# One split instruction for up to four pieces of weights instead of two, in a two-layer decoder trunk on one Trainium2 core

## The chip, the core and the metric

The kernel runs on one core of one Trainium2 chip. The metric is device time in microseconds of one launch, that is, of the whole two-layer trunk for one sequence of 256 tokens. All data are float32 in memory. Engine names in what follows: PE is TensorE (matmuls; PEld are its weight loads), DVE is VectorE, ACT is ScalarE, SP is the engine whose queue issues the transfers here.

## What is computed

The reference is a decoder trunk of two layers, cut here to what matters:

```python
for layer in range(2):
    shift, scale, gate = modulation(c, ada_w[layer])        # matrix-vector products with silu(c)
    h = x * (1 + scale) + shift
    y = rglru_mixer(h)  if layer == 0 else nsa_mixer(h)      # recurrent block / sparse attention
    x = layer_norm(ALPHA * x + (1 + gate) * y)
    # the same once more with y = square(relu(h @ w1)) @ w2
```

Each layer has a mixer with its input and output projections and an MLP of 2048 to 8192 to 2048. There are four sub-layers in all (mixer, MLP, mixer, MLP), each with its own modulation (three products of a 2048-vector with a 2048 by 2048 matrix) and its own layer norm. Some 610 MB of weights are read once each.

## The kernel before

**Weights as a stream.** All weights come as one list of units (`Item`), each 128 partitions by 2048 columns of float32 (1 MB), in the order in which they are needed. `prefetch` (L95 to L107) issues one transfer a unit on SP's queue into one of six raw buffers. `pump` (L109 to L146) takes the next unit that has arrived, and does what its kind asks: a unit of modulation weights ("a") goes through one multiply-and-sum on DVE (L120, 2048 columns) and its buffer is free again; a unit of matmul weights ("w") holds four **pieces** of 512 columns, and is split.

**The split.** A float32 product is made of three matmuls with rounded parts (L193 to L195): high by high, high by low, low by high. So each weight is needed as a high part `whi`, a rounded copy made on ACT (L135), and a low part `wlo`, the rest, made on DVE (L136: raw minus `whi`). Both live in a ring of 16 pieces. The ring has two counters: `prod`, how many pieces have been split, and `cons`, how many PE has used up. A split may be issued when its pieces fit: its last piece may be at most 16 ahead of `cons`. Before the change one pair of instructions makes two pieces (1024 columns), and a unit takes two pairs:

```python
w = min(1024, it.width)
s = it.p0 + 2 * it.group
if s + 2 > self.cons + RING:
    return
```

**Matrix products.** `gemm_ws` takes a piece as the stationary operand (12 matmuls of 256 columns a piece), `gemm_as` the activations (3 matmuls of 512 columns a piece and token tile; there are two token tiles of 128 rows). With `stagger` the first token tile goes over all 16 pieces of a chunk before the second one starts, and only the second gives pieces back to the ring.

**The order of the work.** The program is recorded in one pass: a counter of estimated time decides when `pump` emits a split and when side tasks (normalization, gates, activations) take their next step. A scheduler then orders each engine's instructions, and each engine runs its own in that order. An instruction that waits holds up all that stand behind it on its engine.

**Places named below.**
- `modulate` (L447 to L462): four tiles of 128 features are scaled on ACT (L454), then split like the weights: high part on ACT (L496), low part on DVE (L497). What L454 needs (`hA`, `hB`) comes from L427 to L436 on DVE, right behind the L120s.
- The first sub-layer's input is made in five groups of 4, 4, 4, 2 and 2 feature tiles (`GROUPS0`), the second's in four groups of 4 (`GROUPS1`). Each group has its L120s, then its modulation, then four units of weights (`w_part`); those of the two groups of 2 hold two pieces each. `gemm_ws_outer` runs the group's 16 (or 8) pieces.
- `proj` (L602 to L662) makes the output projections; its `task` multiplies by the gate (L632), adds the residual (L637), takes statistics (L638). `ln_task` (L504 to L572) follows for each token tile: L509, L511 (ACT), L517 to L530, then L534 (ACT) and L540 normalize, L549 transposes on PE, L553 copies (ACT), or L561 and L563 modulate. There are four layer norms; the first ends near 379 us of the profile, the second lies around 1115 to 1141 us, the third around 1544 to 1566 us, the last at the end.

Of the kernel before, what the change touches and what calls it, by code (L numbers as in the profile page):

```python
# [33 lines left out]
NS2 = 6  # L34
LNACT = (0, 2)
# [14 lines left out]
class Builder:  # L50
# [58 lines left out]
    def pump(self):  # L109
        nc = self.nc  # L110
        while self.pi < len(self.items):
# [15 lines left out]
            else:  # L127
                w = min(1024, it.width)
                s = it.p0 + 2 * it.group
                if s + 2 > self.cons + RING:  # L130
                    return
                src = r[:, 1024 * it.group:1024 * it.group + w]
                hi = self.whi[:, s % RING:s % RING + 2, :].rearrange("p a b -> p (a b)")[:, :w]
                lo = self.wlo[:, s % RING:s % RING + 2, :].rearrange("p a b -> p (a b)")[:, :w]
                nc.scalar.activation(hi, src, AF.Copy)  # L135
                nc.vector.tensor_tensor(out=lo, in0=src, in1=hi.bitcast(F32), op=OP.subtract)  # L136
                self.prod = s + 2
                it.group += 1
                if 2 * it.group < it.pieces:
                    continue  # L140
# [45 lines left out]
    def head(self, kind):  # L186
        """The unit that is next in the stream, as it came."""
# [22 lines left out]
    def gemm_ws_outer(self, act, dones, kinds, groups):  # L210
        """Several chunks of columns side by side, a few tiles of the contraction at a time."""
# [14 lines left out]
    def gemm_as(self, act, done, stagger=None, kind="g"):  # L226
# [13 lines left out]
        # the first token tile runs ahead of the second by as many tiles of weights as the ring holds  # L240
# [37 lines left out]
def build(ctx, tc, a, out):  # L278
# [30 lines left out]
    # silu(c), on every partition  # L309
# [112 lines left out]
    def make_ss(s, k0=0, k1=16):  # L422
        """h = zn * hA + hB, with zn the normalized rows before sub-layer s (its input where s is 0)."""
# [20 lines left out]
    def modulate(s, k0, k1, rows, A):  # L444
        """Up to four feature tiles of the transposed rows become the two parts of the modulated ones."""
# [59 lines left out]
    def ln_task(s, z, t, stats, A, fin=None, rows=None):  # L505
        """Normalizes the rows of token tile t and, with A, makes sub-layer s+1's modulated rows, transposed
        (or with rows, the transposed rows alone; or with fin, the last layer norm's w and b, the output)."""
# [400 lines left out]

    tok = [None, None]

    # compressed keys and values
    kc = const.tile([128, 4, 15], F32, name="kc")
    vc = B.t2([15, 4, 128])

# [325 lines left out]
```

## Time and profile before

| | before |
|---|---|
| three runs | 2290.78 us median (2289.36 to 2290.9) |
| the profiled execution | span 2292.0 us, from the first to the last instruction (no other time is listed for it) |
| PE busy | 2198.1 us, 96% |
| DVE busy | 1672.3 us, 73% |
| ACT busy | 1057.2 us, 46% |
| mean granted TensorE clock | 0.987 |
| split instructions | 721 on ACT (L135), 721 on DVE (L136) |
| transfers | 623.95 MB, mean 272 GB/s |

The profile is of one execution. Busy times overlap, so a share says nothing by itself of what a stage waits for. PE's 2198.1 us leave 93.9 us in which PE was idle.

### The profile page before, as it was taken

What the parts mean: (1) busy time and instruction counts of PE and PEld (TensorE: products, weight loads), DVE (VectorE), ACT (ScalarE), POOL (GpSimd) and SP (SyncE); (2) the same over time, 40 slices, a digit from 0 to 9 for tenths busy, and PEclk for the clock granted to TensorE, in tenths of its full rate; (3) what the DMA queues carried; (4) which work ended last, traced back from release to release, by engine and by line L of the source; (5) the groups of instructions that cost most, each with busy time, mean ns of one, the idle gap of its engine ahead of it and who ended that gap; (6) DMA issues with size and microseconds to landing.
All of it is one profiled execution on the core that took longest, in us unless ns stands there. A gap on an engine that the chain in (4) does not pass through costs nothing.

```text
span 2292.0 us, 33881 instructions
## 1 busy us (share of the span) xinstructions
PE 2198.1 (96%) x13970; PEld 1966.2 (86%) x13970; DVE 1672.3 (73%) x1987; ACT 1057.2 (46%) x1383; POOL 0.2 (0%) x4
## 2 busy tenths in 40 slices
PE   4799998989999999999999999999999999999997
PEld 3798977978998998998789988788989989988986
DVE  8899999886777767778887688668766444454456
ACT  2356644364453453444443355536544534443541
POOL 0000000000000000000000000000000000000000
PEclk9899999999999999999999999999999999999999
DMA  9987888988878878788689775356788555555561
GB/s 371 411 331 286 338 328 322 373 346 341 306 302 321 298 273 310 294 302 319 234 292 349 293 272 214 132 192 219 281 308 307 190 190 189 191 184 185 208 250 37
DMA packets 98218, 623.95 MB, mean 272 GB/s; under 512 B 10909, under 2 KB 13405, under 8 KB 26896
## 3 DMA queue, kind: packets, MB, share of 16 engines
q1 hardware_dynamic: 98064, 621.80, 72.5%
q8 instruction: 109, 1.79, 0.3%
q14 instruction: 45, 0.37, 0.0%
HBM read 613.30 MB, written 8.45 MB: 271 GB/s over the span
## 4 chain that ended last, share of the span: by engine, by line
PE 84%; DVE 11%; ACT 2%; issue 2%; DMA 1%; DVEq 0%; SPq 0%; ACTq 0%
PE g L195 26%; PE g L194 26%; PE g L193 26%; DVE raw L120 5%; DVE wlo L136 2%; PE m L1124 1%; PE m L1090 1%; ACT whi L135 1%; DMA raw<-in_lru_in 1%; DVE s L801 1%; PE m L929 1%; PE m L1116 0%; PE m L1127 0%; DVE s L497 0%; ACT s L454 0%
## 5 line engine op out<-in xcount | busy, mean ns | idle before, releaser
L136 DVE TENSOR_TENSOR wlo<-raw,whi 128x1024 fp32r<-128x1024 f32 x721 | 872.1, 1222 | 512.4 <-ACT whi L135 510.9
L135 ACT ACTIVATE whi<-raw 128x1024 fp32r<-128x1024 f32 x721 | 754.7, 1057 | 911.7 <-PE g L195 454.2
L193 PE MATMUL g<-s,whi 128*128 128x256 f32 (+1 forms) x2768 | 781.1, 283 | 51.6 <-ACT s L496 50.0
L194 PE MATMUL g<-s,whi 128*128 128x256 f32 (+1 forms) x2768 | 780.4, 282 | 5.1 <-DVE s L497 5.1
L195 PE MATMUL g<-s,wlo 128*128 128x256 f32 (+1 forms) x2768 | 780.6, 283 | 3.2 <-DVE wlo L136 3.2
L193 PEld LDWEIGHTS g<-s,whi 128*128 128x128 f32 (+1 forms) x2768 | 523.1, 189 | 59.1 <-ACT s L496 53.0
L193 PE MATMUL g<-whi,s 128*128 128x512 f32 x1376 | 547.4, 398 | 5.4 <-ACT s L496 5.4
L194 PE MATMUL g<-wlo,s 128*128 128x512 f32 x1376 | 544.9, 396 | 0.0
L195 PE MATMUL g<-whi,s 128*128 128x512 f32 x1376 | 544.6, 396 | 0.3 <-DVE s L497 0.3
L194 PEld LDWEIGHTS g<-s,whi 128*128 128x128 f32 (+1 forms) x2768 | 525.8, 190 | 8.9 <-DVE s L497 6.8
L195 PEld LDWEIGHTS g<-s,wlo 128*128 128x128 f32 (+1 forms) x2768 | 525.1, 190 | 4.8 <-DVE wlo L136 3.8
L120 DVE SCALAR_TENSOR_TENSOR raw<-raw,one,cond 128x2048 f32<-128x2048 f32 x192 | 447.7, 2345 | 19.1 <-DMA raw<-in_ada 18.9
L193 PEld LDWEIGHTS g<-whi,s 128*128 128x128 f32 x1376 | 258.9, 188 | 70.2 <-ACT s L496 7.4
L195 PEld LDWEIGHTS g<-whi,s 128*128 128x128 f32 x1376 | 258.7, 188 | 64.8 <-DVE s L497 2.2
L194 PEld LDWEIGHTS g<-wlo,s 128*128 128x128 f32 x1376 | 258.9, 188 | 62.0 <-issue 0.8
L454 ACT ACTIVATE s<-s,hB,hA 128x256 f32<-128x256 f32 x32 | 16.7, 590 | 120.9 <-DVE hA L430 80.4
L194 PE MATMUL m<-s,whi 128*128 128x256 f32 x256 | 71.1, 278 | 0.0
L195 PE MATMUL m<-s,wlo 128*128 128x256 f32 x256 | 71.1, 278 | 0.0
L193 PE MATMUL m<-s,whi 128*128 128x256 f32 x256 | 70.8, 279 | 0.2 <-ACT whi L135 0.2
L497 DVE TENSOR_TENSOR s<-t,s 128x512 fp32r<-128x512 f32 x78 | 52.8, 685 | 1.5 <-ACT s L496 1.3
L675 ACT ACTIVATE t<-g 128x512 f32<-128x512 f32 x58 | 33.9, 588 | 34.7 <-PE g L195 34.7
L193 PEld LDWEIGHTS m<-s,whi 128*128 128x128 f32 x256 | 47.8, 188 | 0.5 <-ACT whi L135 0.4
(189 smaller groups left out, 1048.6 us busy)
## 6 DMA issues: line engine op xcount, KB each, us to landing
raw<-in_mlp_w SPq DMA_DIRECT2D x256, 1024.0 KB, 5.0
raw<-in_ada SPq DMA_DIRECT2D x192, 1024.0 KB, 6.6
raw<-in_lru_in SPq DMA_DIRECT2D x28, 1024.0 KB, 8.4
raw<-in_nsa_kv SPq DMA_DIRECT2D x24, 1024.0 KB, 5.3
raw<-in_lru_out SPq DMA_DIRECT2D x16, 1024.0 KB, 6.3
raw<-in_nsa_q SPq DMA_DIRECT2D x16, 1024.0 KB, 6.5
raw<-in_nsa_out SPq DMA_DIRECT2D x16, 1024.0 KB, 4.9
t<-in_lnrow SPq DMA_DIRECT2D x24, 256.0 KB, 6.2
```

The lines of the kernel that those rows point to most:

```text
L120: nc.vector.scalar_tensor_tensor(r, r, self.one, self.cond, op0=OP.mult, op1=OP.mult, accum_out=it.col)
L135: nc.scalar.activation(hi, src, AF.Copy)
L136: nc.vector.tensor_tensor(out=lo, in0=src, in1=hi.bitcast(F32), op=OP.subtract)
L193: mm(out, lhi, rhi, start=start, stop=False, skip_group_check=True)
L194: mm(out, lhi, rlo, start=False, stop=False, skip_group_check=True)
L195: mm(out, llo, rhi, start=False, stop=stop, skip_group_check=True)
L497: V.tensor_tensor(out=lo, in0=src, in1=hi.bitcast(F32), op=OP.subtract)
L675: SC.activation(r2, banks[b], AF.Relu)
L801: V.scalar_tensor_tensor(o[:, sh:], p[:, :256 - sh], tap(i, j), o[:, sh:], op0=OP.mult, op1=OP.add)
L929: T.matmul(hv, r[:, 128 * l:128 * l + 128], x[:, :, h:15 + h, l], start=(h == 0 and l == 0), stop=(h == 1 and l == 15))
L1090: T.matmul(ps, qT[:, h, 128 * t:128 * t + 128], kT[g // 2][:, g % 2, :, 0:K], start=True, stop=True)
L1124: T.matmul(po, vt[br][:, kt, 128 * g:128 * g + 128], pT[:, br, kt], start=first, stop=False)
```

## The change

A constant `WIDE = 4` is new. A split now covers `n` pieces: up to four, but not past the end of the unit and not past the end of the ring. Its instructions are up to 2048 columns wide, and it is issued when all its `n` pieces fit into the ring. (The diff also drops comments, so that line numbers after the change are 1 to 3 higher.)

```diff
+WIDE = 4
...
             else:
-                w = min(1024, it.width)
-                s = it.p0 + 2 * it.group
-                if s + 2 > self.cons + RING:
+
+                s = it.p0 + it.group
+                n = min(WIDE, it.pieces - it.group, RING - s % RING)
+                if s + n > self.cons + RING:
                     return
-                src = r[:, 1024 * it.group:1024 * it.group + w]
-                hi = self.whi[:, s % RING:s % RING + 2, :].rearrange("p a b -> p (a b)")[:, :w]
-                lo = self.wlo[:, s % RING:s % RING + 2, :].rearrange("p a b -> p (a b)")[:, :w]
+                w = min(512 * n, it.width - 512 * it.group)
+                src = r[:, 512 * it.group:512 * it.group + w]
+                hi = self.whi[:, s % RING:s % RING + n, :].rearrange("p a b -> p (a b)")[:, :w]
+                lo = self.wlo[:, s % RING:s % RING + n, :].rearrange("p a b -> p (a b)")[:, :w]
                 nc.scalar.activation(hi, src, AF.Copy)
                 nc.vector.tensor_tensor(out=lo, in0=src, in1=hi.bitcast(F32), op=OP.subtract)
-                self.prod = s + 2
-                it.group += 1
-                if 2 * it.group < it.pieces:
+                self.prod = s + n
+                it.group += n
+                if it.group < it.pieces:
                     continue
```

In the built program the 720 splits of 1024 columns on each engine become 316 of 2048 and 88 of 1024; the one of 768 (`nsa_g`, the attention's branch gates) stays. Of the 88, eight belong to the two small groups of `GROUPS0`. The other 80 come behind `nsa_g`, which has two pieces: from there on every fourth unit lies across the end of the ring and is split in two halves.

The order of the instructions moves with it. First place: **DVE, the first group of the first sub-layer** (`hA` is the modulation's scale, `s` are the activations, `wlo` and `whi` the ring). Before:

```order
L430 TENSOR_SCALAR hA_91<-mod_87 128x4
L136 TENSOR_TENSOR wlo<-raw,whi 128x1024
L497 TENSOR_TENSOR s_224<-s_187,s_223 128x1024
L136 TENSOR_TENSOR wlo<-raw,whi 128x1024 x7
L120 SCALAR_TENSOR_TENSOR raw,mod_87<-raw,one,cond 128x2048 x4
```

and with the change:

```order
L433 TENSOR_SCALAR hA_91<-mod_87 128x4
L139 TENSOR_TENSOR wlo<-raw,whi 128x2048
L500 TENSOR_TENSOR s_224<-s_187,s_223 128x1024
L139 TENSOR_TENSOR wlo<-raw,whi 128x2048 x3
L121 SCALAR_TENSOR_TENSOR raw,mod_87<-raw,one,cond 128x2048 x4
```

The activations' low part still stands behind the first split, which is now twice as wide; ACT's order is the same (L454, one `whi`, L496, the other `whi`). The second and third group, and the third and fourth of the second sub-layer, read alike.

Second place: **DVE, the first layer norm, second token tile** (`z` is named `s` here; L632, L637, L638 and L509 belong to the second tile). Before:

```order
L540 TENSOR_SCALAR s_2895<-s_2895,mv,r 128x512
L136 TENSOR_TENSOR wlo<-raw,whi 128x1024
L632 TENSOR_TENSOR s_2895<-g_2832,s_2546 128x512
L637 SCALAR_TENSOR_TENSOR s_2895<-t_2829,s_2895 128x512
L638 BN_STATS stats_2351<-s_2895 128x6
L509 BN_AGGR mv<-stats_2351 128x2
L517 TENSOR_SCALAR var<-mv 128x1
```

and with the change:

```order
L543 TENSOR_SCALAR s_2807<-s_2807,mv,r 128x512
L139 TENSOR_TENSOR wlo<-raw,whi 128x2048
L635 TENSOR_TENSOR s_2807<-g_2746,s_2478 128x512
L640 SCALAR_TENSOR_TENSOR s_2807<-t_2743,s_2807 128x512
L641 BN_STATS stats_2295<-s_2807 128x6
L512 BN_AGGR mv<-stats_2295 128x2
L139 TENSOR_TENSOR wlo<-raw,whi 128x2048
L520 TENSOR_SCALAR var<-mv 128x1
```

Before, the group's eight narrow splits all stood ahead of the second tile's L632; now three wide ones do, and the fourth stands between its L509 and L517. In the first tile's part, the first narrow split stood between L637 and L638; the first wide one stands behind L638, L509 and L517.

Third place: **DVE, the third layer norm**, from the first low part of the first token tile (L497) to the second tile's gate (L632). Before:

```order
L497 TENSOR_TENSOR s_12652<-t_12646,s_12651 128x4x128
L136 TENSOR_TENSOR wlo<-raw,whi 128x1024
L497 TENSOR_TENSOR s_12672<-t_12666,s_12671 128x4x128
L136 TENSOR_TENSOR wlo<-raw,whi 128x1024
L497 TENSOR_TENSOR s_12689<-t_12683,s_12688 128x4x128
L136 TENSOR_TENSOR wlo<-raw,whi 128x1024
L497 TENSOR_TENSOR s_12708<-t_12702,s_12707 128x4x128
L632 TENSOR_TENSOR s_12607<-g_12558,s_12272 128x512
```

and with the change:

```order
L500 TENSOR_TENSOR s_12210<-t_12204,s_12209 128x4x128
L139 TENSOR_TENSOR wlo<-raw,whi 128x2048
L500 TENSOR_TENSOR s_12230<-t_12224,s_12229 128x4x128
L139 TENSOR_TENSOR wlo<-raw,whi 128x1024
L500 TENSOR_TENSOR s_12247<-t_12241,s_12246 128x4x128
L139 TENSOR_TENSOR wlo<-raw,whi 128x1024
L500 TENSOR_TENSOR s_12264<-t_12258,s_12263 128x4x128
L635 TENSOR_TENSOR s_12167<-g_12118,s_11844 128x512
```

Here one of three narrow splits became a wide one, so 1024 columns more stand between the first low part (L497 before, L500 now) and the second tile's gate (L632 before, L635 now). On ACT, ahead of the first L496 of this norm, three narrow `whi` behind L534 became two wide ones.

## Rows read from the trace of the kernel before

**Rows 1.** Busy time by stretch: stretch, length, engines, PEclk, DMA share, GB/s.
```profile
0.00:160.00 160.00, 111.23 (x804) 103.94 (x805) 141.85 (x200) 56.91 (x76) 0.20 (x4) 0.95 0.95 377
160.00:345.00 185.00, 178.37 (x1141) 161.31 (x1140) 183.24 (x198) 119.28 (x159) 0.00 (x0) 0.99 0.84 316
345.00:480.00 135.00, 116.49 (x792) 109.03 (x791) 122.90 (x148) 53.84 (x68) 0.00 (x0) 0.91 0.86 335
480.00:2292.00 1812.00, 1792.05 (x11239) 1591.97 (x11237) 1224.31 (x1445) 827.21 (x1081) 0.00 (x0) 1.00 0.69 254
1320.00:1480.00 160.00, 159.42 (x1015) 133.01 (x1015) 128.64 (x314) 86.52 (x227) 0.00 (x0) 1.00 0.58 212
```

**Rows 2.** PE's own waits: who waited for whom, us in total, times, longest.
```profile
PE g L193 <- ACT s L496: 55.4, 12, 25.9
PE m L549 <- ACT s L534: 8.7, 3, 3.9
PE g L195 <- DVE wlo L136: 3.2, 3, 2.4
```

**Rows 3.** Groups of instructions by form: busy us, mean ns | idle before, releasers.
```profile
L136 DVE TENSOR_TENSOR wlo<-raw,whi 128x1024 fp32r<-128x1024 f32 x720 | 871.2, 1222 | 511.8 <-ACT whi L135 510.3
L135 ACT ACTIVATE whi<-raw 128x1024 fp32r<-128x1024 f32 x720 | 753.9, 1058 | 911.1 <-PE g L195 454.2 <-PE g L194 381.2 <-DMA raw<-in_lru_in 29.7
L120 DVE SCALAR_TENSOR_TENSOR raw<-raw,one,cond 128x2048 f32<-128x2048 f32 x192 | 447.7, 2345 | 19.1 <-DMA raw<-in_ada 18.9
L497 DVE TENSOR_TENSOR s<-t,s 128x512 fp32r<-128x512 f32 x78 | 52.8, 685 | 1.5 <-ACT s L496 1.3
L496 ACT ACTIVATE s<-t 128x512 fp32r<-128x512 f32 x78 | 47.6, 624 | 0.1
```

**Rows 4.** Timeline, first group of the first sub-layer: start us, us, instruction [idle before].
```profile
37.13 1.04 ACT L135 ACTIVATE whi<-raw 128x1024 fp32r<-128x1024 f32 x1
38.20 1.23 DVE L136 TENSOR_TENSOR wlo<-raw,whi 128x1024 fp32r<-128x1024 f32 x1 [3.09 <-ACT whi L135]
39.02 6.72 ACT L135 ACTIVATE whi<-raw 128x1024 fp32r<-128x1024 f32 x7
40.48 8.03 DVE L136 TENSOR_TENSOR wlo<-raw,whi 128x1024 fp32r<-128x1024 f32 x7
```

**Rows 5.** Timeline, first layer norm: the splits behind the first token tile, L517 of the second.
```profile
362.01 1.06 ACT L135 ACTIVATE whi<-raw 128x1024 fp32r<-128x1024 f32 x1 [11.54 <-PE g L195]
363.41 1.06 ACT L135 ACTIVATE whi<-raw 128x1024 fp32r<-128x1024 f32 x1 [0.34 <-PE g L195]
...
363.10 1.23 DVE L136 TENSOR_TENSOR wlo<-raw,whi 128x1024 fp32r<-128x1024 f32 x1 [1.07 <-ACT whi L135]
364.24 0.69 DVE L638 BATCH_NORM_STATS2 stats<-s 128x6 f32<-128x512 f32 x1
...
377.29 0.15 DVE L517 TENSOR_SCALAR var<-mv 128x1 f32<-128x1 f32 x1
```

**Rows 6.** Timeline, groups of the second sub-layer: DVE's waits at the splits.
```profile
404.97 1.23 DVE L136 TENSOR_TENSOR wlo<-raw,whi 128x1024 fp32r<-128x1024 f32 x1 [1.10 <-ACT whi L135]
407.89 1.23 DVE L136 TENSOR_TENSOR wlo<-raw,whi 128x1024 fp32r<-128x1024 f32 x1 [1.70 <-ACT whi L135]
...
467.33 1.23 DVE L136 TENSOR_TENSOR wlo<-raw,whi 128x1024 fp32r<-128x1024 f32 x1 [0.70 <-ACT whi L135]
```

**Rows 7.** Timeline, third layer norm: PE's wait in the second token tile.
```profile
1569.55 0.50 PE L193 MATMUL g<-whi,s 128*128 128x512 f32 x1 [0.69 <-ACT s L496]
```

**Rows 8.** Busy time by stretch of L136 alone: stretch, length, DVE busy (count), PEclk, DMA, GB/s.
```profile
0.00:160.00 160.00, 37.37 (x32) 0.95 0.95 377
160.00:345.00 185.00, 72.32 (x62) 0.99 0.84 316
345.00:480.00 135.00, 40.33 (x34) 0.91 0.86 335
1320.00:1480.00 160.00, 37.11 (x31) 1.00 0.58 212
```

## The prediction

> **What bounds the kernel now.** I read first the busy time by stretch [rows 1]. PE's columns give its idle time: 160.00 - 111.23 = 48.8 us in the first stretch (0 to 160), 6.6 in the second (160 to 345), 18.5 in the third (345 to 480) and 20.0 in the 1812 us that follow. So for four fifths of the span PE is the bound, and DVE, busy 1224 of 1812 us there, may save microseconds that no one collects. Only 73.9 us ahead of 480 and 20.0 behind it are open to a change that leaves the matmuls alone. The second view is PE's own waits [rows 2]: 55.4 us for the activations' high part (L496), 8.7 us for a layer norm (L534), but only 3.2 us for a split low part. PE seldom waits for a split as such. It waits for the short chains that make the next activations, and these stand on ACT and DVE between the splits. The third view is the cost of the splits by form [rows 3]: on both engines nearly all the idle time ahead of a split is a wait, DVE's for `whi`, ACT's for PE to give pieces back. Last I read the timelines at those chains [rows 4 to 7].
>
> **What a wide split costs.** No instruction of before is a 2048-column split, so its time comes from two widths of alike work. On DVE 512 columns take 685 ns (L497) and 1024 take 1222 (L136), so 512 more cost 537, and 2048 take 1222 + 2 x 537 = 2296 ns. On ACT 624 and 1058 give 434 for 512, and 2048 take 1926 ns [rows 3]. The nearest bound above is L120, which works through 2048 columns in 2345. Two narrow ones don't cost 2 x 1222 = 2444 in a row, for they overlap: seven took 8.03 us on DVE, a pitch of (8.03 - 1.22)/6 = 1.135, and 6.72 on ACT, 0.943 [rows 4]. The second half of a wide one adds 1.074 and 0.868. So a pair merged saves 0.061 us on DVE and 0.075 on ACT. Without overlap it would save DVE 2444 - 2296 = 148 ns, the upper end.
>
> The 316 merged pairs take 316 x 0.061 = 19 us off DVE. Of these pairs some 60 lie ahead of 480 us: 32 narrow low parts up to 160 of which eight stay, 62 and 34 behind them [rows 8], so 12 + 31 + 17. The rest lie under PE. I price the saving there at nothing: the work that hides it is PE's, which uses a piece in about 1.5 us (1812 us for the other 592 narrow splits, two pieces each), while up to 12 of 16 pieces, some 18 us of matmuls, stand ready when a unit of four is split. A wide pair takes 1.9 + 2.3 us. If that cover went, each unit would cost PE up to 4.2 us, and the waits for low parts, 3.2 us now, would show it.
>
> **What it costs where the cover is thin.** Where a chain waits for the first split of a group, it now waits for all four pieces: `whi` ends 0.868 later, and what stands behind `wlo` on DVE, the activations' low part among it, another 1.074 later.
>
> *First three groups, first sub-layer (0 to 160).* DVE sits idle until the first `whi` (3.09 us ahead of 38.20) and then works without a gap [rows 4]. It starts 0.87 later and wins 4 x 0.061 = 0.24 back over the group's four units: +0.63. The next group's L120s queue behind it, and PE waits for them by way of L454 and L496. Three groups: **+1.9**. The lower end is 0, since DMA is 95% busy there [rows 1] and L120 waits 18.9 us for its data [rows 3]. The upper is 3 x 1.94 = 5.8, if PE feels both delays in each group.
>
> The Trainium skill ("Perfetto Trace Analysis", section "Optimizing Scalar/DVE Operations") has a rule that speaks against the change: where Scalar or Vector are not saturated but cause bubbles on other engines, breaking up instructions may let work complete sooner. By it all fronts below would be losses; the 3.09 us for which DVE sits idle agree with it.
>
> *Recurrent block (160 to 345).* DVE is busy 183.24 of 185 us. Some 7 merged pairs lie on its chain to the stretch's end: **-0.4**. The ends are -1.9 (31 x 0.061) and +1, a wide split ahead of one short operation.
>
> *First layer norm and second sub-layer (345 to 480).* The first split behind the first token tile had to wait for two pieces, until 362.01; the second for two more, until 363.41 [rows 5]. A wide one waits for four: +1.40, and its `whi` is 0.87 longer. Against that L638 (0.69) and one L517 (0.15) now run in the gap instead of behind the split, and four units win 0.24: **+1.2** (0.9 to 1.7). In the second group DVE waits twice for `whi`, 1.10 and 1.70 us [rows 6]. Each wait becomes 0.87 longer, less 0.24: **+1.5**; PE is still at work on the group before, but the third group's L120s queue behind it. The third group is like those above: **+0.6**. In the fourth DVE waits 0.70 for `whi` ahead of the low part [rows 6], and PE's own start hangs on both: 0.87 + 1.07, less some 0.2 of first matmuls that need no low part: **+1.7**. Together **+5.0**. The ends: 1.0, if PE and DMA (86% busy) hide all but one front, and 7.
>
> *Second and third layer norm.* In the second, three splits leave the first tile's chain and as many columns come to stand ahead of the second tile's gate: **0** (-0.9 to +1). In the third PE already waits 0.69 us for the second tile's L496 [rows 7], so a delay of that chain goes straight to PE. The first tile's L496 comes later by the longer `whi` ahead of it, 0.87, and 1024 more columns stand ahead of L632, 1.07: **+1.9** (0 to 3). The last norm has no splits beside it.
>
> Sum: 1.9 - 0.4 + 5.0 + 0 + 1.9 = **+8.4 us**. The profiled span of 2292.0 becomes 2300.4. That execution is 1.2 us longer than the median 2290.78, so on the median the forecast is **2299.2 us**. A measurement of this kernel can tell about 0.2%, 4.6 us, from no change; slower begins at 2295.4, faster below 2286.2.
>
> **Rivals.**
>
> *The fronts are hidden.* For it: the DMA share is 0.95, 0.84 and 0.86 in the three early stretches [rows 1], and L120 waits for data [rows 3]; if a late unit of weights ends most groups, DVE's 0.6 us matter to nobody, and a chain that starts late only turns idle time behind it into work. Against it: L120's waits are 18.9 us, PE's for L496 are 55.4. With the lowest ends of the early groups, 0 + 1.0, and about 1 from the third norm: 2290.78 + 2 = about 2293, no difference.
>
> *Grouping pays (the other side).* The place is 160 to 345 us and the groups of DVE work about it, where DVE is saturated, 183.24 of 185 [rows 1]. If narrow splits don't overlap there, since L120s and other operations stand between them, each pair saves 148 ns: 60 x 0.148 = 8.9 us, and if the fronts cost less than some 2 us, the time is 2290.8 - 8.9 + 2 = about 2284. It decides from about 6.6 us of net gain. Against it: PE is idle for only 6.6 us in the stretch where DVE is full, the seven splits in a row show the overlap plainly, and in the other two stretches DVE waits just where the split became longer.
>
> Such a rule is in the Trainium skill too (the same page and section): grouping into larger operations can improve throughput if the engine is saturated. DVE's 183.24 of 185 us fit its condition, PE's 20.0 us of idle time behind 480 leave it nothing there.
>
> *Attention suffers too.* From 1320 to 1480 us PE is busy 159.42 of 160 us, and DVE 128.64 [rows 1], with 31 narrow splits among its short chains [rows 8]. About 15 wide ones take their place; if half of these stand ahead of a chain that PE needs, 7 or 8 x 1.07 = some 8 us on top: about 2307. Against it: PE has only 0.6 us of waits there, so something else has covered chains that already stood behind 1.22 us splits and 2.35 us L120s.
>
> That the change does less than it says I leave out: the built program has 316 wide splits.
>
> **How the numbers follow.** The forecast, 2295.4 to 2306 with the fronts in full or for the most part, 0.55. Fronts hidden 0.27. Grouping pays 0.10. Attention suffers 0.08. Slower by over 0.2%: 0.55 + 0.08 = 0.63; within 0.27; faster 0.10. The ends of the terms add up to 0 - 1.9 + 1.0 - 0.9 + 0 = -1.8 and 5.8 + 1 + 7 + 1 + 3 = 17.8, but five ends do not come together; I take 2289.0 (the low ends) to 2306.0, which leaves out the faster rival, the worse one, and little else: about 2 in 10.
>
> **What would show it.** In the changed profile: L136's successor at 2048 columns near 2296 ns on DVE and 1926 on ACT; more than 2345 would mean that each unit costs more than two narrow splits. PE's idle time from 0 to 480 us should grow from 73.9 to about 80.4, with PE's wait for L496 up from 55.4; behind 480 from 20.0 to about 22. DVE's wait ahead of the first low part of a group should grow from 3.09 to about 3.96. In the first norm, the first wide `whi` should start where the second narrow one did, 1.4 us later. PE's waits for low parts should stay near 3.2. The forecast is wrong if the groups end at the same time as before although their first split ends later (then DMA or L120 ended them), if PE's idle time shrinks between 160 and 345 by more than 2 us, or if PE idles between 1320 and 1480.

## The result, and the profile after the change

The change made the kernel slower, by about half a per cent: 2302.73 us (2301.98 to 2305.72, four runs) against 2290.84 us, ratio 1.0053, 95% interval 1.0038 to 1.0067. Beside other runs of before it was measured once more (e8 below): 2301.85 us against 2291.73, ratio 1.0044 (1.0031 to 1.0057), which is +10 us. The forecast was 2299.2 us, from 2289.0 to 2306.0, and slower with 0.63. The profiled execution took 2301.98 us with a span of 2300.2; the forecast for the span was 2300.4.

Busy time by stretch of the changed kernel, with the columns of [rows 1]:

```profile
0.00:160.00 160.00, 110.94 (x796) 103.64 (x797) 139.21 (x185) 55.19 (x62) 0.20 (x4) 0.94 0.96 377
160.00:345.00 185.00, 178.18 (x1138) 161.90 (x1137) 181.63 (x170) 114.74 (x129) 0.00 (x0) 0.98 0.83 312
345.00:480.00 135.00, 113.56 (x752) 105.15 (x751) 117.32 (x128) 51.16 (x51) 0.00 (x0) 0.89 0.86 330
480.00:2300.20 1820.20, 1799.22 (x11289) 1597.41 (x11288) 1202.74 (x1192) 787.49 (x826) 0.00 (x0) 1.00 0.70 253
```

DVE is less busy in every stretch, ACT too, and PE is idle longer: 49.1, 6.8, 21.4 and 21.0 us instead of 48.8, 6.6, 18.5 and 20.0. These windows cut at fixed times and the later ones hold work that had been in the one before, so the delays below tell more. No window cuts the whole span: PE was idle for 93.9 us of it before and for 98.3 with the change. The cost of the splits by form, as in [rows 3]:

```profile
L139 DVE TENSOR_TENSOR wlo<-raw,whi 128x2048 fp32r<-128x2048 f32 x316 | 722.3, 2290 | 480.6 <-ACT whi L138 480.4
L138 ACT ACTIVATE whi<-raw 128x2048 fp32r<-128x2048 f32 x316 | 603.6, 1915 | 817.9 <-PE g L198 393.0 <-PE g L197 359.3 <-DVE s L626 11.0
```

A wide split takes 2290 ns on DVE and 1915 on ACT (forecast 2296 and 1926). PE's own waits, beside [rows 2] (L196 to L198 are what L193 to L195 were, L499 was L496, L552 was L549, L537 was L534):

```profile
PE g L196 <- ACT s L499: 57.4, 10, 26.7
PE m L552 <- ACT s L537: 9.0, 2, 6.9
PE g L196 <- ACT whi L138: 6.3, 7, 1.1
PE g L198 <- DVE wlo L139: 4.0, 1, 4.0
PE g L197 <- DVE s L500: 1.3, 1, 1.3
```

The last row stands for this one of before:

```profile
PE g L194 <- DVE s L497: 5.1, 6, 1.5
```

The wait for the activations' high part grew from 55.4 to 57.4. The third row, seven waits of about 1 us for a high part, is new but for one wait of 0.5 us. In exchange these waits for the activations' low part, six in before, came down to one. Now the timeline of the first group, beside [rows 4]:

```profile
37.20 1.89 ACT L138 ACTIVATE whi<-raw 128x2048 fp32r<-128x2048 f32 x1
39.95 5.50 ACT L138 ACTIVATE whi<-raw 128x2048 fp32r<-128x2048 f32 x3
...
39.13 2.29 DVE L139 TENSOR_TENSOR wlo<-raw,whi 128x2048 fp32r<-128x2048 f32 x1 [3.94 <-ACT whi L138]
42.47 6.69 DVE L139 TENSOR_TENSOR wlo<-raw,whi 128x2048 fp32r<-128x2048 f32 x3
```

DVE idles 3.94 us ahead of the group's first low part, not 3.09; the forecast said 3.96. Three wide ones in a row take 6.69 us, a pitch of (6.69 - 2.29)/2 = 2.20, against 2 x 1.135 = 2.27 for narrow pairs: 0.07 each, where 0.061 was forecast. The first layer norm, beside [rows 5], then the second group of the second sub-layer, beside [rows 6], and the third norm, beside [rows 7]:

```profile
365.99 1.91 ACT L138 ACTIVATE whi<-raw 128x2048 fp32r<-128x2048 f32 x1 [12.08 <-PE g L198]
...
367.94 2.29 DVE L139 TENSOR_TENSOR wlo<-raw,whi 128x2048 fp32r<-128x2048 f32 x1 [2.11 <-ACT whi L138]
...
406.69 2.29 DVE L139 TENSOR_TENSOR wlo<-raw,whi 128x2048 fp32r<-128x2048 f32 x1 [1.84 <-ACT whi L138]
...
414.29 1.23 DVE L500 TENSOR_TENSOR s<-s,s 128x1024 fp32r<-128x1024 f32 x1 [2.69 <-ACT s L499]
...
1562.30 0.50 PE L196 MATMUL g<-whi,s 128*128 128x512 f32 x1 [1.17 <-ACT s L499]
1577.69 0.50 PE L196 MATMUL g<-whi,s 128*128 128x512 f32 x1 [1.74 <-ACT s L499]
```

The first of the two waits of the third norm, in before:

```profile
1555.39 0.51 PE L193 MATMUL g<-whi,s 128*128 128x512 f32 x1 [0.65 <-ACT s L496]
```

PE's work is 2.58 us late when it comes to the first norm, so 365.99 answers to 363.41, to the hundredth where the second narrow split had started. In the second group DVE waits 1.84 and 2.69 us instead of 1.10 and 1.70, 1.73 more in all, where the forecast had 2 x 0.87. But they are not the same waits. The split at 406.69 now stands ahead of the modulation's `hA` and `hB` (L437 to L439), which in before were done by 402.73, ahead of the first of these waits; and the second wait is that of the activations' low part for its high part. In the third norm the second tile's wait is 1.74 instead of 0.69.

Since PE executes the same 13970 matmuls in both kernels, each can be matched by name and occurrence, and the difference of the two start times is PE's delay. This table gives what the delay grows by in each stretch (stretches by the times of before; worked out from the traces, each kernel against the profile of before):

| us, by stretch | to 165 | to 345 | to 490 | to 1165 | to 1310 | to 1545 | to 1600 |
|---|---|---|---|---|---|---|---|
| the change | +1.84 | +0.74 | +4.79 | -1.62 | -0.73 | +1.37 | +1.75 |
| the change again (e8) | +1.58 | +1.30 | +4.32 | -1.62 | 0.00 | +0.70 | +1.74 |
| before again (e4) | +0.13 | +0.14 | -0.62 | +0.66 | -0.87 | +0.17 | +0.01 |
| narrow groups (e1) | -0.03 | +1.80 | +0.56 | -1.62 | -0.88 | +1.37 | +1.73 |
| wide groups only (e2) | +1.82 | 0.00 | +4.05 | -0.80 | -0.15 | -0.36 | -0.58 |
| pairs (e3) | +0.18 | +0.36 | -0.40 | -1.00 | -1.00 | +1.33 | -0.58 |
| wide on ACT (e5) | +2.64 | +0.52 | +5.15 | +0.01 | +0.80 | +0.84 | +3.35 |
| wide on DVE (e6) | +1.82 | -0.81 | +3.50 | +1.33 | -0.97 | +0.42 | +2.73 |
| short first unit (e7) | +2.55 | +2.37 | -0.84 | -1.02 | -0.88 | +0.18 | +0.01 |
| first unit narrow (e9) | +0.40 | +0.40 | +1.70 | -1.44 | -0.74 | +1.44 | +1.73 |
| wide recurrent block (e10) | +0.23 | +2.35 | +0.66 | -0.99 | -0.88 | +0.74 | +0.03 |
| wide MLPs (e11) | +0.16 | +0.16 | +0.20 | -1.00 | -0.88 | +0.74 | +0.03 |
| 512 columns (e12) | +3.46 | +1.26 | +1.05 | -1.03 | -1.17 | +0.44 | +0.11 |

Each row is one execution. The two of before differ by up to 0.9 us in a stretch, so a smaller difference between two rows says little. From 490 to 1600 us the kernels e10 and e11, which are narrow through both norms and attention, gain 1.1 us on the profile of before, but so they do on e4, the same kernel profiled again. That 1.1 us lies in the second norm, at the transposes of its second token tile. In before, e4 and e11:

```profile
1141.51 3.38 PE L549 MATMUL m<-ident,s 128*128 128x128 f32 x16 [2.86 <-ACT s L534]
1141.36 3.11 PE L549 MATMUL m<-ident,s 128*128 128x128 f32 x16 [2.86 <-ACT s L534]
1142.22 1.97 PE L560 MATMUL m<-ident,s 128*128 128x128 f32 x16 [2.86 <-ACT s L545]
```

After the same wait of 2.86 us the same 16 transposes take 3.38 or 3.11 us in before and 1.97 in e11, and in the change too. TensorE's granted clock has two levels, 1.2 and 2.4 GHz, and PEclk is its mean as a share of the higher one. From 1137 to 1160 us it is 0.85 in before, 0.78 in e4, 0.93 in e11 and in the change. Why it fell ahead of these transposes in some kernels and not in others is not shown.

### The profile page after: what moved, and what is told of

It is laid out like the page before. It is cut to its first block, busy times and chain, and to the rows that moved or that the text cites. A ratio compares the mean times of both kernels' runs of the same rounds, so it can differ in the third digit from the quotient of the medians.

```text
span 2300.2 us, 32804 instructions
## 1 busy us (share of the span) xinstructions
PE 2201.9 (96%) x13970; PEld 1968.1 (86%) x13970; DVE 1640.9 (71%) x1671; ACT 1008.6 (44%) x1067; POOL 0.2 (0%) x4
## 4 chain that ended last, share of the span: by engine, by line
PE 85%; DVE 10%; ACT 2%; issue 2%; DMA 1%; DVEq 0%; SPq 0%; ACTq 0%
PE g L198 26%; PE g L197 26%; PE g L196 26%; DVE raw L121 5%; DVE wlo L139 2%; PE m L1127 1%; PE m L1093 1%; ACT whi L138 1%; PE m L197 1%; PE m L198 1%; PE m L196 1%; PE m L932 1%; DMA raw<-in_ada 1%; PE m L843 0%; PE g L843 0%
## 5 line engine op out<-in xcount | busy, mean ns | idle before, releaser
L139 DVE TENSOR_TENSOR wlo<-raw,whi 128x2048 fp32r<-128x2048 f32 (+1 forms) x405 | 827.4, 2055 | 516.2 <-ACT whi L138 514.3
L138 ACT ACTIVATE whi<-raw 128x2048 fp32r<-128x2048 f32 (+1 forms) x405 | 697.2, 1726 | 897.7 <-PE g L198 431.4
L196 PE MATMUL g<-s,whi 128*128 128x256 f32 (+1 forms) x2768 | 782.0, 284 | 57.4 <-ACT s L499 51.1
L198 PE MATMUL g<-s,wlo 128*128 128x256 f32 (+1 forms) x2768 | 780.3, 282 | 4.0 <-DVE wlo L139 4.0
L196 PEld LDWEIGHTS g<-s,whi 128*128 128x128 f32 (+1 forms) x2768 | 524.0, 190 | 65.4 <-ACT s L499 53.8
L196 PE MATMUL g<-whi,s 128*128 128x512 f32 x1376 | 547.6, 398 | 6.8 <-ACT s L499 6.3
L198 PE MATMUL g<-whi,s 128*128 128x512 f32 x1376 | 544.5, 396 | 0.9 <-DVE s L500 0.9
L198 PEld LDWEIGHTS g<-s,wlo 128*128 128x128 f32 (+1 forms) x2768 | 525.7, 190 | 5.1 <-DVE wlo L139 4.2
L196 PEld LDWEIGHTS g<-whi,s 128*128 128x128 f32 x1376 | 258.7, 188 | 71.6 <-ACT s L499 8.1
L198 PEld LDWEIGHTS g<-whi,s 128*128 128x128 f32 x1376 | 258.7, 188 | 66.2 <-DVE s L500 4.0
L198 PE MATMUL m<-s,wlo 128*128 128x256 f32 x256 | 71.3, 279 | 0.0
L196 PE MATMUL m<-s,whi 128*128 128x256 f32 x256 | 70.8, 280 | 0.0
L678 ACT ACTIVATE t<-g 128x512 f32<-128x512 f32 x58 | 33.9, 589 | 55.4 <-PE g L198 55.4
L500 DVE TENSOR_TENSOR s<-t,s 128x512 fp32r<-128x512 f32 x78 | 51.9, 687 | 6.6 <-ACT s L499 6.3
L499 ACT ACTIVATE s<-t 128x512 fp32r<-128x512 f32 x78 | 47.7, 628 | 0.9
```

What stands on the lines that cost most here:

```text
L196: mm(out, lhi, rhi, start=start, stop=False, skip_group_check=True)
L198: mm(out, llo, rhi, start=False, stop=stop, skip_group_check=True)
L499: SC.activation(hi, src, AF.Copy)
L500: V.tensor_tensor(out=lo, in0=src, in1=hi.bitcast(F32), op=OP.subtract)
L678: SC.activation(r2, banks[b], AF.Relu)
```

## The experiments

The theory after the result: the loss sits where a chain waits for the first split of a group, in the first two sub-layers and the third norm. Rivals: every wide split costs a little, since four pieces must be free; the width costs on DVE, not on ACT; and, still, grouping may pay where DVE is full.

**e1, narrow groups.** The units of both grouped sub-layers are split 1024 columns at a time, all others as in the change.

```diff
-                n = min(WIDE, it.pieces - it.group, RING - s % RING)
+                n = min(2 if it.part in (1, 3) else 4, it.pieces - it.group, RING - s % RING)
```

> Edit: units of the groups of the first two sub-layers (GROUPS0 and GROUPS1) are split 1024 columns at a time as before, all others 2048 as in the change. Theory (fronts: the cost sits where a chain waits for a group's first split): the terms of the groups and the first norm, 1.9 + 5.0, go; what stays is the recurrent block, the second and third norm and attention, by the trace of the change +0.7 - 1.8 + 0.6 + 1.8 = +1.3, so about 2292 us, ratio 1.0006. Rival (every wide split costs PE a little, since 4 of 16 pieces must be free): about 9 in 10 wide splits are still there, so most of the 11.9 us stays, 2300 or more, ratio over 1.004.

Measured: 2297.19 us against 2292.25, ratio 1.0025 (1.0015 to 1.0035), +5 us. Half of the loss is gone, less than the theory said, and far more than the rival's tenth. The table shows the first and third stretch near zero. The third norm keeps its loss; PE's waits there are those of the change:

```profile
1557.10 0.50 PE L197 MATMUL g<-whi,s 128*128 128x512 f32 x1 [1.17 <-ACT s L505]
1572.49 0.50 PE L197 MATMUL g<-whi,s 128*128 128x512 f32 x1 [1.74 <-ACT s L505]
```

**e2, wide groups only.** The complement.

```diff
+                n = min(4 if it.part in (1, 3) else 2, it.pieces - it.group, RING - s % RING)
```

> Edit: the complement; only the units of GROUPS0 and GROUPS1 are split 2048 columns at a time, all others 1024. Theory (fronts): 1.9 + 5.0 = +6.9, about 2297.7 us, ratio 1.0030. Rival (every wide split costs): about 1 in 10 of 11.9, so 2292, ratio 1.0005. If the fronts cost more than forecast (the timed difference was 11.9, that of the two profiles 8.2): up to 2301, ratio 1.0045.

Measured: 2296.51 us, ratio 1.0022 (1.0013 to 1.0031), +4.3. A tenth of the wide splits carries some two fifths of the loss. In the trace it has the fronts in full, +1.82 and +4.05.

**e3, pairs.** Four pieces are admitted together, and made by two narrow instructions on each engine.

```diff
-                nc.scalar.activation(hi, src, AF.Copy)
-                nc.vector.tensor_tensor(out=lo, in0=src, in1=hi.bitcast(F32), op=OP.subtract)
+                for c in range(0, w, 1024):
+                    nc.scalar.activation(hi[:, c:min(c + 1024, w)], src[:, c:min(c + 1024, w)], AF.Copy)
+                for c in range(0, w, 1024):
+                    nc.vector.tensor_tensor(out=lo[:, c:min(c + 1024, w)], in0=src[:, c:min(c + 1024, w)], in1=hi[:, c:min(c + 1024, w)].bitcast(F32), op=OP.subtract)
```

> Edit: a unit's four pieces are admitted together as in the change, but made by two instructions of 1024 columns on ACT and two on DVE. Theory (the width of the instruction costs, for what waits for it waits for all of it): as before, ratio 1.000 within 0.001, about 2291. Rival (what costs is that four pieces of the ring must be free before a split is recorded): 2299 to 2303, ratio 1.004 to 1.005.

Measured: 2292.48 us, ratio 1.0006 (0.9997 to 1.0014). The condition at recording time costs nothing that can be told. In the built program the scheduler puts these narrow instructions, outside attention, into nearly the order of before: the waits follow the data, and half a unit can again be made as soon as two pieces are free. It is the width of the instruction that costs, together with the order that the scheduler makes of wide ones.

**e4, before again.** No edit.

> Edit: none, the kernel of before once more, timed against itself and profiled again. Expected of every theory: ratio 1.000, the interval at most 0.001 to either side. Its profile tells whether the span of 2292.0 us, on which the sum was made, is a usual one: by the median of the times, less the 1.8 us by which a time lies above its span in the run of the change, it should be about 2289; then some 3 us of the difference of 11.9 lie in the profile that was chosen and not in the change.

Measured: ratio 1.0000 (0.9991 to 1.0009). Eleven executions of one program went from 2288.28 to 2296.46 us, and the median of 30 runs of before beside them was 2292.25. The profiled one took 2293.46 us with a span of 2291.7, so the span of the record, 2292.0, was that of a longer execution than the middle one, as expected, though by 1.5 us rather than 3.

**e5, wide on ACT alone.** Low parts by two instructions of 1024 columns.

```diff
-                nc.vector.tensor_tensor(out=lo, in0=src, in1=hi.bitcast(F32), op=OP.subtract)
+                for c in range(0, w, 1024):
+                    nc.vector.tensor_tensor(out=lo[:, c:min(c + 1024, w)], in0=src[:, c:min(c + 1024, w)], in1=hi[:, c:min(c + 1024, w)].bitcast(F32), op=OP.subtract)
```

> Edit: ACT makes the high parts of four pieces in one instruction as in the change, DVE the low parts in two instructions of 1024 columns as before. Theory (fronts, and most of it by ACT: a chain starts 0.87 us later behind a wide whi, and without wide low parts DVE wins nothing back): first sub-layer 3 x 0.87 = +2.6, first norm 1.4, second group 1.7, third and fourth 0.87 each = +4.9, third norm +0.9: +8, about 2300, ratio 1.0036. Rival (the cost is DVE's: wide low parts stand ahead of the activations' low parts and the norm's gate): +2, ratio 1.001.

Measured: 2304.88 us, ratio 1.0056 (1.0044 to 1.0069), +13. The theory's +8 was short, the rival's +2 is out: wide high parts alone cost as much as the whole change. The first group of its trace, DVE:

```profile
39.13 1.22 DVE L140 TENSOR_TENSOR wlo<-raw,whi 128x1024 fp32r<-128x1024 f32 x1 [3.94 <-ACT whi L138]
41.40 8.03 DVE L140 TENSOR_TENSOR wlo<-raw,whi 128x1024 fp32r<-128x1024 f32 x7
```

DVE idles the same 3.94 us and wins nothing back: the eight narrow ones end 0.27 us later than the four wide ones (49.43 against 49.16). The third norm costs this version 3.35 us, more than the change's 1.75. PE's two waits there are those of the change, but the granted clock is not. Busy time by stretch, of e5, then of the change:

```profile
1577.00:1592.00 15.00, 13.23 (x59) 10.18 (x58) 9.65 (x18) 11.87 (x19) 0.00 (x0) 0.89 0.01 4
1577.00:1592.00 15.00, 14.31 (x72) 11.71 (x73) 12.00 (x13) 13.21 (x17) 0.00 (x0) 1.00 0.32 116
```

A clock of 0.89 for 15 us is worth 1.65 us, about the 1.60 between the two. In e6 it is 0.89 there as well. So part of what these two versions lose is clock, and not the width itself.

**e6, wide on DVE alone.** High parts by two instructions.

```diff
-                nc.scalar.activation(hi, src, AF.Copy)
+                for c in range(0, w, 1024):
+                    nc.scalar.activation(hi[:, c:min(c + 1024, w)], src[:, c:min(c + 1024, w)], AF.Copy)
```

> Edit: the complement; two instructions of 1024 columns on ACT as before, one of 2048 on DVE. In the built program the activations' low part now stands ahead of the first wide split of a group. Theory (fronts, most by ACT): the group's DVE work ends when it did, less 0.2 for each group; the third norm's gate still has 1024 columns more ahead, +1.07: between -0.5 and +2 in all, about 2293, ratio 1.0004. Rival (the cost is DVE's): +6 or more, ratio over 1.0026.

Measured: 2301.84 us, ratio 1.0039 (1.0026 to 1.0053), +10. By the expectation's numbers the rival won, but its reason did not: no activation's low part stands behind a wide split here. The group's start shows what was overlooked:

```profile
38.94 1.22 DVE L501 TENSOR_TENSOR s<-s,s 128x1024 fp32r<-128x1024 f32 x1 [4.03 <-ACT s L500]
40.09 8.89 DVE L140 TENSOR_TENSOR wlo<-raw,whi 128x2048 fp32r<-128x2048 f32 x4
```

With the wide low part waiting for two high parts, the scheduler lets the activations' low part go first. That waits for ACT's L500, which comes behind the first high part, and DVE idles 4.03 us, about as long as with a wide `whi`. Whatever DVE starts with, it idles some 0.9 us longer than the 3.09 of [rows 4]. The first stretch grows by 1.82 us, as in the change.

**e7, a short first unit.** From before; the first unit behind each group's modulation is made 512 columns at a time.

```diff
+                n = min(1 if it.lead else 2, it.pieces - it.group, RING - s % RING)
```

> Edit: from the kernel of before, the first unit of weights behind each group's modulation is split 512 columns at a time, all others 1024 as before: the change the other way round, at the fronts alone. Theory (fronts): whi ahead of the activations 1058 - 624 = 0.43 us shorter, four small pairs cost DVE 4 x 0.598 - 2 x 1.135 = 0.12 more: first sub-layer 3 x -0.31 = -0.9, first norm and second and third group about -0.4 each, fourth group -0.43 - 0.54 = -1.0: -3, ratio 0.9987, faster than both kernels. Rival (what matters is DVE's sum of work, which grows): +0.9, ratio 1.0004.

Measured: 2295.50 us, ratio 1.0017 (1.0008 to 1.0025), slower by 3.8. The gain at the start is there, and the expectation was still wrong:

```profile
37.88 0.69 DVE L140 TENSOR_TENSOR wlo<-raw,whi 128x512 fp32r<-128x512 f32 x1 [2.66 <-ACT whi L139]
39.97 8.70 DVE L140 TENSOR_TENSOR wlo<-raw,whi 128x512 fp32r<-128x512 f32 x9
```

DVE idles 2.66 us instead of 3.09, as forecast, and PE starts the first three groups 0.32, 0.28 and 0.22 us earlier than before. But PE's delay grows by 2.55 us up to 165 and by 2.37 more up to 345; then only 0.84 comes back. The first loss comes at the fourth group, the first of the two small ones. In before DVE makes its `hA` ahead of the splits, at 139.03; here two short splits stand ahead of it, and it comes at 140.09. PE starts the group 1.04 us late. Then the clock falls, which it did not in before. Busy time by stretch, of before, then of e7:

```profile
140.00:152.00 12.00, 10.23 (x82) 9.63 (x81) 10.03 (x19) 8.14 (x14) 0.00 (x0) 1.00 1.00 407
140.00:152.00 12.00, 9.81 (x69) 9.40 (x68) 7.35 (x14) 6.65 (x11) 0.00 (x0) 0.86 1.00 417
```

0.14 of 12 us is 1.7 us of clock. What it loses behind 165 us is not taken apart here. So e7 does not show that a shorter first split loses by itself.

**e8, the change again.**

> Edit: none, the change once more, beside the runs of before on this chip. The first comparison gave ratio 1.0053 (1.0038 to 1.0067) from four runs each; the two partial versions gave 1.0025 and 1.0022. If the parts add up: 1.0047. If they hide or feed each other: 1.0035 or less, or 1.0055 or more. By the profiles (8.2 us): 1.0036.

Measured: 2301.85 us, ratio 1.0044 (1.0031 to 1.0057), near the sum of the two parts, 1.0047. The parts add up within their intervals.

**e9, first unit narrow.** As in the change, but the unit that e7 made short is split 1024 columns at a time; 309 of 316 wide splits stay.

```diff
+                n = min(2 if it.lead else WIDE, it.pieces - it.group, RING - s % RING)
```

> Edit: as in the change, but the first unit behind each group's modulation is split 1024 columns at a time; 309 of 316 wide splits stay. Theory (a group's end is the end of DVE's chain, and DVE idles longer only ahead of the group's first split): the fronts of both groups' sub-layers vanish but for one 0.7 in the second group, so about what narrow groups altogether gave, +3 to +5, ratio 1.0013 to 1.0022. Rival (all wide splits of a group cost, not the first): about the change's +10, ratio 1.0044.

Measured: 2297.51 us, ratio 1.0025 (1.0013 to 1.0036), +5. Seven splits fewer do as much as all the groups narrow (e1). The first group, DVE:

```profile
38.31 1.23 DVE L140 TENSOR_TENSOR wlo<-raw,whi 128x1024 fp32r<-128x1024 f32 x1 [3.10 <-ACT whi L139]
42.01 6.70 DVE L140 TENSOR_TENSOR wlo<-raw,whi 128x2048 fp32r<-128x2048 f32 x3 [0.20 <-ACT whi L139]
```

The idle time is 3.10 us again, three of four units are wide, and the first stretch grows by 0.40 instead of 1.84.

**e10, wide in the recurrent block only,** where DVE is full.

```diff
+                n = min(4 if it.part == 2 else 2, it.pieces - it.group, RING - s % RING)
```

> Edit: only the 32 units of the recurrent block and its output (160 to 345 us, where DVE is busy 183 of 185) are split 2048 columns at a time, all others 1024. Forecast of the record: -0.4 (-1.9 to +1). Rival of the record (grouping pays where DVE is saturated): -1.9 to -4.6, ratio 0.9992 to 0.998. By the trace of the change (PE's wait for a low part there grew from 2.4 to 4.0): +0.7 to +1, ratio 1.0004.

Measured: 2292.70 us against 2292.58, ratio 1.0005 (0.9996 to 1.0014). The rival that grouping pays there by 0.1 to 0.2% is out. PE's waits in the block:

```profile
187.26 0.38 PE L197 MATMUL g<-s,whi 128*128 128x256 f32 x1 [1.07 <-ACT whi L139]
192.00 0.58 PE L199 MATMUL g<-s,wlo 128*128 128x256 f32 x1 [4.01 <-DVE wlo L140]
283.03 0.50 PE L197 MATMUL g<-whi,s 128*128 128x512 f32 x1 [1.65 <-ACT s L859]
```

The longest wait for a low part was 2.4 us [rows 2]; it is 4.01 now. DVE is busy for 180.16 us of the block instead of 183.24, and PE collects none of it. In the profile PE's delay grows by 2.35 us in the block; 0.76 of this is there at 230 us, and most of the rest comes with the wait of 1.65 us at 283, where PE did not wait in before.

**e11, wide in the MLPs only,** behind their first 16 units: 196 wide splits.

```diff
+                n = min(4 if it.part == 4 else 2, it.pieces - it.group, RING - s % RING)
```

> Edit: only the 196 wide splits of the two MLPs behind their first 16 units are made, all other splits are 1024 columns wide; DVE's busy time falls by about 12 us, ACT's by about 15. Theory (PE covers them, and no chain waits there): nothing, ratio 1.000 within 0.001. Rival (every wide split costs, since 12 instead of 14 pieces may be ready): 196 of 316 of 10 us, +6, ratio 1.0027.

Measured: 2293.11 us, ratio 0.9999 (0.9991 to 1.0008). Three fifths of the change, at no price and for no gain. The page's first part, then PE's wait for low parts:

```profile
PE 2200.1 (96%) x13970; PEld 1968.0 (86%) x13970; DVE 1648.6 (72%) x1791; ACT 1025.8 (45%) x1187; POOL 0.2 (0%) x4
```

```profile
PE g L199 <- DVE wlo L140: 2.4, 1, 2.4
```

DVE's busy time fell by 23.7 us (from 1672.3) and ACT's by 31.4, more than expected: 0.12 us a pair on DVE and 0.16 on ACT, where 0.061 and 0.075 were forecast. That pairs apart from each other save more is the likely reason, but it was not tested. None of it shows in the time.

**e12, 512 columns everywhere.**

```diff
-WIDE = 4
+WIDE = 1
```

> Edit: every split is 512 columns wide, the change the other way round. Theory (fronts shorter by 0.43, DVE's work longer by 0.061 for each old split of 1024): groups -1.3 + 1.5 + -1.0, third norm -1, recurrent block up to +3.8 as DVE is full there; +0 to +4, ratio 1.000 to 1.0018. Rival (breaking up lets work complete sooner wherever an engine causes bubbles on PE): -3, ratio 0.9987. What the 512-column splits at the groups' heads showed (+3.8 with 24 units made so) speaks for the upper end or more.

Measured: 2298.02 us, ratio 1.0026 (1.0015 to 1.0036), +5.4, a little above the expected end. (In e7 it was one unit in each of nine groups that was made so, not 24.) DVE's busy time rises by 71.8 us, and from 160 to 345 it is 184 of 185 (the page's first part, then busy time by stretch):

```profile
PE 2199.1 (96%) x13970; PEld 1964.3 (86%) x13970; DVE 1744.1 (76%) x2708; ACT 1180.2 (51%) x2104; POOL 0.2 (0%) x4
```

```profile
160.00:345.00 185.00, 178.12 (x1137) 161.08 (x1136) 184.01 (x256) 125.93 (x221) 0.00 (x0) 0.98 0.80 303
```

The largest loss, +3.46, comes up to 165 us. The first three groups start at -0.30, +0.17 and +0.66 us against before: half a microsecond is lost with each, as eight splits more than before would have it (8 x 0.061 = 0.49). The rest comes at the fourth group, where the clock falls as in e7 (0.86 from 140 to 152). So the split of 1024 columns is the best of the three widths here: narrower lengthens DVE's own work where that ends a group, wider costs idle time ahead of the chains. No version beat before.

## Why the prediction was right, and where it was off

**The bound and the cover: right.** PE covers the splits of the steady stretches: from 490 to 1100 us and from 1600 us to the end the change's delay does not grow by more than 0.3 us, and e11 shows it by itself.

**The price of a wide split: right** to 0.6 per cent (2290 and 1915 ns). The saving was too small: DVE's busy time fell by 31.4 us (1672.3 to 1640.9), where the forecast had 19, about 0.10 us a pair. Nothing hung on it, since PE covers most of the pairs.

**The first three groups, +1.9: right,** +1.84 and +1.58. PE starts the three groups 0.92, 1.51 and 2.10 us later (first L193 at 39.17, 71.54 and 103.90; first L196 at 40.09, 73.05 and 106.00), 0.6 more with each, as the term says. That the group's first split is the cause is shown by e9, which changes that unit alone. That DVE's idle time ahead of it counts, rather than the width of one of the two instructions, is borne out by e5 and e6: both keep one engine narrow, both have the idle time (3.94, 4.03), and up to 165 us they lose +2.64 and +1.82, the change +1.84.

The Trainium skill's rule from "Perfetto Trace Analysis", section "Optimizing Scalar/DVE Operations", that breaking up may help where Scalar or Vector are not saturated but cause bubbles on other engines, agrees with e9 against the change (2297.5 and 2301.9 us). Carried below 1024 columns it gains nothing here: e7 and e12 are 3.8 and 5.4 us slower than before. The other rule of that section, that grouping can improve throughput if the engine is saturated, shows no gain in e10, which widens the splits where before DVE was busy for 183 of 185 us.

**The first norm and the second sub-layer, +5.0: right in sum,** +4.79 and +4.32. The norm gave +0.97 (L549 at 379.63, L552 at 383.18, less the 2.58 carried in), forecast +1.2. At the third group's head the sum is 3.04 (435.86 and 441.48), where the norm, the second group and the third group's own 0.87 make 3.6; at the fourth's it is 3.62 (468.30 and 474.50), where 4.2 were due. So the second group gave 1.2 instead of 1.5, by other waits than the forecast named, and the third its 0.6. Behind the fourth's head +1.2 came, where 0.8 was due. There PE did not wait for the activations' low part behind a wide `wlo`, as the step had it. It waits 1.00 us for the second unit's high part, in place of 0.65 for the low part: the new row among PE's waits. At least part of the rest of that 1.2 belongs to the execution of before: from 477 to 487 us it starts 90 matmuls, e4 starts 87, and the change starts 87 in the same time at the place that answers to it (see the last section). That the terms add up to +4.8 where +5.0 was forecast is in part luck.

**The recurrent block, -0.4: wrong in sign,** +0.74 and +1.30. The step took 7 merged pairs' savings as gained on DVE's chain and kept a wide split ahead of one short operation for the other end. PE's wait for one low part grew from 2.4 to 4.0 us, but other waits ended with it: behind it, at 230 us, the delay has grown by only 0.37. The rest comes at waits for activations that PE did not have there before, 0.44 us at 283.04 (L853) and 1.04 us at 310.62 (L499), while one of 1.37 us at 304.31 is gone. Alone the block costs more in the profiles, +2.35 in e10, so the terms do not simply add up. The timed runs of e10 cannot tell this from nothing.

**The second norm, 0: right within its ends.** PE's delay falls by 1.9 us there in the profile of the change. 1.4 of this is the clock at the 16 transposes (3.38 us before, 1.97 with the change), which has nothing to do with the splits of this norm, since e11, narrow there, has the 1.97 too. PE's idle time falls by 0.5.

**The third norm, +1.9: right,** +1.75 and +1.74. The second tile's wait grew by 1.05 (forecast 1.07), the first tile's by 0.52 (forecast 0.87). The reading that 1024 more columns on DVE do the former is not shown: e5, with narrow low parts, has that wait at 1.73 as well.

**The sum, +8.4:** +8.2 between the profiles, +10 to +12 in timed runs. The forecast range held them. What is short is not one term. The forecast put the profiled execution 1.2 us above the median, comparing a span with times; since a time lies 1.8 us above its span, it was 3.0 above. The profiled execution of the change lies 0.75 below its median, and 8.2 + 3.0 + 0.7 are the 11.9 of the first comparison. So the gap between profiles and timed runs is a matter of which executions were profiled, and that 8.2 meets 8.4 so closely is in part luck. Of the timed loss not all is located: e1, which leaves the groups out, is still +5 us, of which its trace places 1.7 in the third norm and up to 1.8 in the recurrent block; the intervals, 2 us to either side, leave the remainder open.

**What the forecast left out: the clock.** It put the whole sum into PE's idle time, from 73.9 to 80.4 us up to 480 and from 20.0 to about 22 behind. These came as 77.3 and 21.0. Over the whole span PE's idle time is 93.9 us in before and 92.3 in e4, 98.3 in the change and 99.9 in e8. The rest is PE's busy time for the same 13970 matmuls: 2198.1 and 2199.4 us against 2201.9 and 2200.2. The granted clock of the early stretches is lower with the change, and the second profiles, e4 and e8, agree with the first (0.91 and 0.89 from 345 to 480):

```profile
345.00:480.00 135.00, 115.76 (x799) 108.15 (x799) 122.28 (x148) 54.22 (x69) 0.00 (x0) 0.91 0.86 335
345.00:480.00 135.00, 112.51 (x754) 104.08 (x753) 117.60 (x128) 51.17 (x51) 0.00 (x0) 0.89 0.85 329
```

PE stands idle for 6 us and more at the heads of several groups there, so the longer waits and the lower clock come together. How much the clock adds is not separated by any run. Where a chain sets PE's next start, slower matmuls only take the place of idle time: at 141.85 before waits 1.55 us, the change works without a wait, and it is still 1.84 us late behind that.

**The rivals.** Hidden fronts: out, by e9 and by the group heads above. Grouping pays: out, by e10. (Its bar of 6.6 us was the gain ahead of the fronts' 2; net it was 4.6.) Attention suffers: between 1310 and 1545 us the change's delay grew by 1.37 and 0.70, e11's, narrow there, by 0.74, so nothing like 8 us, and PE is busy for 159.71 of the 160 us from 1320 to 1480.

## What to carry to other kernels

Making an instruction wider moves its end for whoever waits first: price the front of each dependent chain (0.87 us of additional idle time on DVE here) against the little that a merged pair saves (0.07 to 0.12 us), and count only savings in stretches where that engine ends the work. In a kernel whose other engine is busy 96% of the time, look for the few splits that stand first behind a stage, seven here, rather than at the 316. When one experiment keeps one engine as it was, look at the built order and at what the engine now starts with: its idle time ahead of the group's first work was nearly the same, 3.94 to 4.03 us, in the change, e5 and e6. And read PE's granted clock beside its waits before a difference of 1 or 2 us is put down to a wait: in the second norm, in e5 and in e7 it was the clock in good part.

## What was not expected of the hardware

PE does not always work through the same matmuls at the same pace. From 1584 to 1650 us two of the traces (e2 and e3) win 2.46 us on before, with no wait in either. Busy time by stretch, first of e3, then of before:

```profile
1600.00:1640.00 40.00, 40.00 (x355) 40.00 (x355) 28.30 (x27) 22.37 (x27) 0.00 (x0) 1.00 0.82 291
```

```profile
1600.00:1640.00 40.00, 40.00 (x342) 40.00 (x341) 27.93 (x27) 21.39 (x27) 0.00 (x0) 1.00 0.78 277
```

PE is busy for the whole of it, at a granted clock of 1.00 in both, and starts 355 or 342 matmuls of 256 columns, one in 113 or in 118 ns. Nearly all such stretches of these traces have the slower pace; which one a stretch takes is not explained by any run here. Seven stretches of this kind and about this length lie in each execution, and eleven executions of one program spread over 8 us (e4): this may be part of it, but that was only argued.
